# Two tokens side by side instead of sixteen: the layout of the one-hot rows that the PEER pick weights are built from

## The chip, the cores and the metric

The kernel runs on one core of a Trainium2 chip. The metric is the time of one execution in device microseconds; the kernel before takes 2791.45 us (median of 3 runs, 2790.54 to 2801.08). Engines are named as the profile names them: PE is TensorE's matmuls, PEld its weight loads, DVE is VectorE, ACT is ScalarE, POOL is GpSimd, SP issues DMAs.

## The reference, cut to what matters

Two layers run over 384 tokens: 256 prompt tokens and 128 sample tokens. Each layer is attention followed by a PEER block, and the change lies in the PEER block of the prompt tokens.

```python
def one(xb):                                   # xb: tokens x 1024
    q = (xb @ w_pq).reshape(m, 8, 2, 64)
    s1 = einsum('nhd,hkd->nhk', q[:, :, 0], k1); s2 = einsum('nhd,hkd->nhk', q[:, :, 1], k2)
    v1, i1 = top_k(s1, 16); v2, i2 = top_k(s2, 16)
    cand = v1[..., :, None] + v2[..., None, :]
    cid = i1[..., :, None] * 128 + i2[..., None, :]
    sc, pick = top_k(cand.reshape(m, 8, 256), 16)
    eid = take_along_axis(cid.reshape(m, 8, 256), pick)   # 8 x 16 experts of 16384 for each token
    g = softmax(sc)
    a = gelu(einsum('nhkd,nd->nhk', u_tab[eid], xb))
    return einsum('nhk,nhkd->nd', g * a, v_tab[eid])
```

An expert's number is `eid = 128*i1 + i2`. For the 256 prompt tokens the kernel computes all 16384 experts densely and multiplies them with a weight matrix G (expert x token) that is zero where a token did not pick an expert. G is what the changed code builds.

## The kernel before

**The PEER block of a layer.** The sample tokens gather their rows: 128 indirect DMAs of rows of `peer_u` and 128 of `peer_v`, 128 x 1024 fp32 each (`gather_slots`, L841), each followed by one DVE instruction on the row (L846 for u, L849 for v); four row buffers. The prompt tokens go through all experts in 64 steps `pb` of 256 experts. A step has a first half (`plain_first` L877 for pb 0 to 15, `first` for the others): load 1 MB of u, multiply with the normed tokens, gelu. Its second half (`second`) multiplies the result by G on DVE (L933), loads 1 MB of v and accumulates the product in four PSUM banks. Most operands are split in two fp32r parts on ACT (L149) and DVE (L152), and every product takes three matmuls (L155 to L157).

**The build of G.** `build(es, tb)` makes G for two groups `es` of 16 columns of `i2`-values (32 columns) and one block `tb` of 16 tokens (`TB = 16`). There are 8 groups, so 4 x 16 = 64 builds in a layer. The 128 picks of a token (8 heads x 16) lie on the 128 partitions. For one token, the left operand A[p, i] is 1 where pick p has `i1 = i`, the right operand B[p, j] is the gate of pick p where `i2 = j`, and A^T B is the token's 128 x 32 piece of G, one matmul (two in fact, B having a high and a low fp16 part: index `i` of the loop). So a build is 32 pairs of a weight load (128 columns of A, fp16) and a matmul that streams 32 columns of B (L910), all into one PSUM bank, which two ACT instructions copy to G (L913).

A is made in one of two ways, given by the table `ACT_ROWS`: in 30 of the 64 builds of a layer by ACT, one `Square` of (2 x id - 2 x i1) per token (L889, 16 of them) and one `Relu` over all (L891), in 34 by one DVE comparison over all 16 tokens (L895). B is always made by DVE: one comparison (L897) and two multiplications by the two parts of the gate (L900).

**The layout.** `iota_r` holds the ids 0 to 127, each repeated 16 times (`[128, 128, TB]`). A tile made by DVE has the shape (id, token): one token's ids are 16 fp16 elements apart, 32 bytes. B always has this shape. A tile made by ACT has the shape (token, id), so one token's 128 ids lie side by side, but ACT reads the ids themselves from `iota_r[:, :, 0]`, 32 bytes apart. The pattern with which a weight load or a matmul reads A and B is `A[:, :, t0 + t]` and `Bt[:, i, :, t0 + t]`.

**What runs around it.** Builds of group pair (0, 1) come first, between the `plain_first` steps 10 to 15. Then `run` walks the 64 steps; in each it does `second(pb)`, the `first` of a later step, then the builds that `BUILDS` gives (pair (2, 3): 16 builds over steps 8 to 15, two per step; (4, 5) and (6, 7): one per step over steps 16 to 47), then some gathered rows (48 by step 16, 256 by step 64). The Tile framework's scheduler decides the final order of the instructions on each engine, and inserts the waits. Tiles: A has two halves in `As`, B two buffers, the PSUM tile of a build is one of three (`at`).

Of the kernel before, what the change touches and what calls it, by code (L numbers as in the profile page):

```python
# [76 lines left out]
def tile_stream_encoder(ctx: ExitStack, tc: tile.TileContext, I, O, stop=None):  # L77
# [546 lines left out]
    def pick(l, hT, hS, kp, dst, after):  # L624
# [95 lines left out]
        def ids(t):  # L720
# [96 lines left out]
    class Experts:  # L817
# [62 lines left out]

        def build(self, es, tb):

            ts = slice(tb * TB, tb * TB + TB)
            dst, L, n = self.dst, self.L, 16 * len(es)
            A = self.As[:, tb % 2 * 1024:tb % 2 * 1024 + 1024].bitcast(F16)
            if tb in ACT_ROWS[es[0]]:

# [17 lines left out]
            m = TB if n * TB <= 512 else TB // 2  # L905
            for t0 in range(0, TB, m):
                ps = at(f"{L}_gp{es[0]}{tb}{t0}")
                for t in range(m):
                    for i in range(2):
# [1 line left out]
                pv = ps[:, :m * n].rearrange("p (t i) -> p i t", t=m)
                for j, e in enumerate(es):
                    S.activation(self.G[e][:, :, tb * TB + t0:tb * TB + t0 + m], pv[:, j * 16:j * 16 + 16], AF.Copy,  # L913
                                 scale=1.0 / GSCALE)
# [164 lines left out]
```

## Time and profile before

| what | value |
|---|---|
| time, median of 3 runs | 2791.45 us (2790.54 to 2801.08) |
| the profiled execution | 2796.06 us, its span 2794.3 us |
| PE busy / DVE busy / ACT busy / POOL busy | 2632.9 / 2170.9 / 1552.8 / 833.0 us |
| mean granted clock of TensorE | 0.962 |
| moved by DMA | 640.14 MB, mean 229 GB/s |

Busy time is the union of an engine's instructions; a matmul's record includes the time it takes to drain, so a busy PE is not a PE at its peak. The profile divides the span in 40 slices of 70 us. The PEER block of the first layer lies at about 430 to 1400 us, that of the second at about 1820 to 2794 us; builds run from 535 to 1220 us and from 1923 to 2610 us.

### The profile page before, as it was taken

Reading aid. Unit: us, or ns where it says so; the run is one execution under the profiler, and the core shown is the slowest. Engines: PE = TensorE matmul, PEld = TensorE weight load, DVE = VectorE, ACT = ScalarE, POOL = GpSimd, SP = SyncE. Lnnn points to the kernel's source line nnn. Section 1 sums busy time; section 2 is a strip of 40 time slices with the busy share of each in tenths; the row PEclk is TensorE's granted clock in tenths of the full one; section 3 lists DMA queues with packets and bytes.
Section 4 is the critical chain, followed back from the end, with each engine's and each line's share of the span. In section 5 each row is a group of like instructions: output and inputs, shape, how many; then the busy total and the mean of one; then the engine's idle time right before and its main releaser. Section 6 shows DMA issues by size and latency. Waiting matters only on the chain.

```text
span 2794.3 us, 45301 instructions
## 1 busy us (share of the span) xinstructions
PE 2632.9 (94%) x17316; PEld 2239.0 (80%) x17316; DVE 2170.9 (78%) x4346; ACT 1552.8 (56%) x2594; POOL 833.0 (30%) x585
## 2 busy tenths in 40 slices
PE   7989998898999999999988989979989999999998
PEld 6767876786789999997876669767857899999987
DVE  6754569967789899998767445698677898989986
ACT  4344333463778888843434443325627788888433
POOL 1000101224334454465210001012243344445651
PEclk9999999999899999999999989999899999999999
DMA  4243532567689888899633343326686888888995
GB/s 164 87 126 109 148 115 76 221 247 291 228 292 331 308 318 317 318 334 353 232 106 103 114 153 115 106 91 234 226 294 233 293 328 307 323 310 320 350 343 198
DMA packets 172010, 640.14 MB, mean 229 GB/s; under 512 B 20880, under 2 KB 37008, under 8 KB 139024
## 3 DMA queue, kind: packets, MB, share of 16 engines
q1 hardware_dynamic: 98064, 368.77, 37.1%
q0 software_dynamic: 73728, 268.47, 26.6%
q8 instruction: 136, 2.23, 0.3%
q14 instruction: 82, 0.67, 0.1%
HBM read 631.48 MB, written 5.70 MB: 228 GB/s over the span
## 4 chain that ended last, share of the span: by engine, by line
PE 62%; DVE 14%; issue 10%; DMA 7%; POOL 4%; ACT 3%; POOLq 0%; SPq 0%; ACTq 0%; DVEq 0%
DMA l0x_row<-in_peer_v_dram,l0e_eid 4%; PE l1x_gp L910 3%; PE l0x_gp L910 3%; PE l1x_acc L156 3%; PE l1x_H L155 3%; PE l1x_acc L157 3%; PE l1x_acc L155 3%; PE l1x_H L157 3%; PE l1x_H L156 3%; PE l0x_acc L156 2%; PE l0x_H L155 2%; PE l0x_acc L157 2%; PE l0x_acc L155 2%; PE l0x_H L157 2%; PE l0x_H L156 2%
## 5 line engine op out<-in xcount | busy, mean ns | idle before, releaser
L841 POOL DMA_INDIRECT l1x_row<-in_peer_v_dram,l1e_eid x128 | 219.6, 1715 | 186.5 <-DVE x_s L849 171.7
L841 POOL DMA_INDIRECT l0x_row<-in_peer_v_dram,l0e_eid x128 | 218.4, 1706 | 187.9 <-DVE x_s L849 166.4
L841 POOL DMA_INDIRECT l1x_row<-in_peer_u_dram,l1e_eid x128 | 161.5, 1261 | 332.9 <-DVE l1x_row L846 295.1
L841 POOL DMA_INDIRECT l0x_row<-in_peer_u_dram,l0e_eid x128 | 161.2, 1259 | 329.3 <-DVE l0x_row L846 289.1
L157 PE MATMUL l0x_H<-l0e_h,l0x_u_l 128*128 128x256 f32 x768 | 219.7, 286 | 4.5 <-DVE l0x_u_l L152 4.3
L155 PE MATMUL l1x_H<-l1e_h,l1x_u_h 128*128 128x256 f32 x768 | 221.8, 289 | 0.0
L155 PE MATMUL l0x_H<-l0e_h,l0x_u_h 128*128 128x256 f32 x768 | 221.7, 289 | 0.0
L157 PE MATMUL l1x_H<-l1e_h,l1x_u_l 128*128 128x256 f32 x768 | 219.3, 285 | 2.5 <-DVE l1x_u_l L152 2.4
L156 PE MATMUL l1x_H<-l1e_h,l1x_u_h 128*128 128x256 f32 x768 | 218.9, 285 | 0.0
L156 PE MATMUL l0x_H<-l0e_h,l0x_u_h 128*128 128x256 f32 x768 | 218.8, 285 | 0.0
L889 ACT ACTIVATE l0x_As<-iota_r,l0e_ni 128x128 f16<-128x128 f16 x480 | 216.8, 541 | 0.0
L889 ACT ACTIVATE l1x_As<-iota_r,l1e_ni 128x128 f16<-128x128 f16 x480 | 216.6, 538 | 0.0
L156 PE MATMUL l0x_acc<-l0x_v_l,l0x_ch 128*128 128x512 f32 x464 | 184.1, 397 | 9.9 <-DVE l0x_v_l L152 9.9
L156 PE MATMUL l1x_acc<-l1x_v_l,l1x_ch 128*128 128x512 f32 x464 | 184.6, 398 | 9.2 <-DVE l1x_v_l L152 9.2
L155 PE MATMUL l1x_acc<-l1x_v_h,l1x_ch 128*128 128x512 f32 x464 | 184.7, 398 | 4.4 <-ACT l1x_v_h L149 4.4
L155 PE MATMUL l0x_acc<-l0x_v_h,l0x_ch 128*128 128x512 f32 x464 | 184.2, 397 | 3.8 <-ACT l0x_v_h L149 3.8
L157 PE MATMUL l1x_acc<-l1x_v_h,l1x_cl 128*128 128x512 f32 x464 | 182.7, 394 | 0.0
L849 DVE SCALAR_TENSOR_TENSOR x_s<-l0x_row,l0x_act,x_s 128x1024 f32<-128x1024 f32 x128 | 165.4, 1292 | 21.9 <-DMA l0x_row<-in_peer_v_dram,l0e_eid 21.2
L157 PE MATMUL l0x_acc<-l0x_v_h,l0x_cl 128*128 128x512 f32 x464 | 182.0, 392 | 0.0
L849 DVE SCALAR_TENSOR_TENSOR x_s<-l1x_row,l1x_act,x_s 128x1024 f32<-128x1024 f32 x128 | 164.0, 1281 | 20.0 <-DMA l1x_row<-in_peer_v_dram,l1e_eid 19.0
L149 ACT ACTIVATE l0x_v_h<-l0x_v 128x1024 fp32r<-128x1024 f32 x116 | 121.3, 1052 | 95.3 <-DMA l0x_v<-in_peer_vt_dram 50.8
L149 ACT ACTIVATE l1x_v_h<-l1x_v 128x1024 fp32r<-128x1024 f32 x116 | 121.2, 1052 | 95.2 <-DMA l1x_v<-in_peer_vt_dram 51.2
(528 smaller groups left out, 7693.6 us busy)
## 6 DMA issues: line engine op xcount, KB each, us to landing
l0x_u_raw<-in_peer_ut_dram SPq DMA_DIRECT2D x64, 1024.0 KB
l0x_v<-in_peer_vt_dram SPq DMA_DIRECT2D x64, 1024.0 KB
l1x_u_raw<-in_peer_ut_dram SPq DMA_DIRECT2D x64, 1024.0 KB
l1x_v<-in_peer_vt_dram SPq DMA_DIRECT2D x64, 1024.0 KB
l_g_raw<-in_w_in_dram SPq DMA_DIRECT2D x16, 1024.0 KB
l_pa_raw<-in_w_in_dram SPq DMA_DIRECT2D x8, 1024.0 KB
l_kbT<-in_cache_b_kT_dram SPq DMA_DIRECT2D x16, 512.0 KB
l_cvb<-in_cache_b_vt_dram SPq DMA_DIRECT2D x16, 512.0 KB
```

The lines of the kernel that those rows point to most:

```text
L149: op = S.activation(hi, src, AF.Copy)
L155: PE.matmul(out, lh, rh, start=start, stop=False)
L156: PE.matmul(out, lh, rl, start=False, stop=False)
L157: PE.matmul(out, ll, rh, start=False, stop=stop)
L841: G.indirect_dma_start(out=row, out_offset=None, in_=self.tables[which], in_offset=bass.IndirectOffsetOnAxis(ap=self.dst["eid"][:, s:s + 1 ...
L849: V.scalar_tensor_tensor(x[2], row, act[:, s:s + 1], x[2], op0=ALU.mult, op1=ALU.add)
L889: S.activation(A[:, t * 128:t * 128 + 128], iota_r[:, :, 0], AF.Square, scale=2.0, bias=dst["ni1"][:, tb * TB + t:tb * TB + t + 1])
L910: PE.matmul(ps[:, t * n:t * n + n], A[:, :, t0 + t], Bt[:, i, :, t0 + t], start=i == 0, stop=i == 1)
```

## The change

The ids are kept in three tiles: `iota_1`, each id once; `iota_2`, each id twice; `iota_16`, ids 0 to 15, sixteen times each, for one comparison in `ids` that read them from `iota_r`. POOL fills them at the start, 128 + 256 + 256 elements in place of 2048. DVE's A and B now have the shape (pair of tokens, id, token of the pair): one token's ids are 2 fp16 elements apart, 4 bytes. The ids are read as one run of 256 (or 64) elements, once for each of the 8 pairs; the tokens' own ids or gates (`pairs`) as runs of 2 elements, each run read 128 (or 32) times. ACT reads its ids from `iota_1`, side by side, and writes as before. The number of instructions and their shapes stay the same. The loop over halves of a block falls away; with 32 columns it ran once.

```diff
-    iota_r = cp.tile([128, 128, TB], F16, name="iota_r")
-    G.tensor_copy(iota_r, iota[:, :, None].to_broadcast([128, 128, TB]))
+    iota_1 = cp.tile([128, 128], F16, name="iota_1")
+    G.tensor_copy(iota_1, iota)
+    iota_2 = cp.tile([128, 128, 2], F16, name="iota_2")
+    G.tensor_copy(iota_2, iota[:, :, None].to_broadcast([128, 128, 2]))
+    iota_16 = cp.tile([128, 16, 16], F16, name="iota_16")
+    G.tensor_copy(iota_16, iota[:, 0:16, None].to_broadcast([128, 16, 16]))
...
-            V.tensor_tensor(ge, every(row[:, :, None, :]), every(iota_r[:, None, 0:16, :]), ALU.is_ge)
+            V.tensor_tensor(ge, every(row[:, :, None, :]), every(iota_16[:, None]), ALU.is_ge)
...
+            def pairs(v, m):
+                return (v[:, tb * TB:tb * TB + TB].rearrange("p (c a) -> p c a", a=2)[:, :, None, :]
+                        .to_broadcast([128, NP, m, 2]))
             if tb in ACT_ROWS[es[0]]:
                 for t in range(TB):
-                    S.activation(A[:, t * 128:t * 128 + 128], iota_r[:, :, 0], AF.Square, scale=2.0,
+                    S.activation(A[:, t * 128:t * 128 + 128], iota_1, AF.Square, scale=2.0,
                                  bias=dst["ni1"][:, tb * TB + t:tb * TB + t + 1])
...
             else:
-                A = carve(A, (128, TB))
-                V.tensor_tensor(A, iota_r, dst["i12"][:, 0, None, ts].to_broadcast([128, 128, TB]), ALU.is_equal)
-            Bt = carve(self.gp.tile([128, 2 * 48 * TB], F16, name=f"{L}_B{es[0]}{tb}", tag="B"), (2, n, TB))
-            V.tensor_tensor(Bt[:, 1], iota_r[:, es[0] * 16:es[0] * 16 + n, :],
-                            dst["i12"][:, 1, None, ts].to_broadcast([128, n, TB]), ALU.is_equal)
+                A = carve(A, (NP, 128, 2))
+                V.tensor_tensor(A, iota_2[:, None].to_broadcast([128, NP, 128, 2]), pairs(dst["i12"][:, 0], 128),
+                                ALU.is_equal)
+                first = [A[:, t // 2, :, t % 2] for t in range(TB)]
+            Bt = carve(self.gp.tile([128, 2 * 48 * TB], F16, name=f"{L}_B{es[0]}{tb}", tag="B"), (2, NP, n, 2))
+            V.tensor_tensor(Bt[:, 1], iota_2[:, None, es[0] * 16:es[0] * 16 + n, :].to_broadcast([128, NP, n, 2]),
+                            pairs(dst["i12"][:, 1], n), ALU.is_equal)
             for i in range(2):
-                V.tensor_tensor(Bt[:, i], Bt[:, 1], dst["gp"][:, i, None, ts].to_broadcast([128, n, TB]), ALU.mult)
+                V.tensor_tensor(Bt[:, i], Bt[:, 1], pairs(dst["gp"][:, i], n), ALU.mult)
...
-                        PE.matmul(ps[:, t * n:t * n + n], A[:, :, t0 + t], Bt[:, i, :, t0 + t], start=i == 0, stop=i == 1)
+                    PE.matmul(ps[:, t * n:t * n + n], first[t], Bt[:, i, t // 2, :, t % 2], start=i == 0, stop=i == 1)
```

The scheduler's order of instructions hardly moves. The first place is ACT's queue among the builds of pair (0, 1) in the first layer. `l0x_As` is A, `iota_r` and then `iota` are the ids, `l0x_G<-l0x_gp` the copy of a build's PSUM bank to G, `l0e_co` the gelu of a step, and "x5" five instructions of one form in a row. Before:

```order
L891 ACTIVATE l0x_As_4340<-l0x_As_4340 128x2048
L913 ACTIVATE l0x_G_4346<-l0x_gp_4560 128x16x16
L913 ACTIVATE l0x_G_4347<-l0x_gp_4560 128x16x16
L913 ACTIVATE l0x_G_4346<-l0x_gp_4600 128x16x16
L913 ACTIVATE l0x_G_4347<-l0x_gp_4600 128x16x16
L889 ACTIVATE l0x_As_4340<-iota_r,l0e_ni_3046 128x128 x5
L879 ACTIVATE l0e_co_3040<-l0x_H_4635 128x512
L889 ACTIVATE l0x_As_4340<-iota_r,l0e_ni_3046 128x128 x3
```

And the same place of the changed kernel:

```order
L901 ACTIVATE l0x_As_4344<-l0x_As_4344 128x2048
L924 ACTIVATE l0x_G_4350<-l0x_gp_4564 128x16x16
L924 ACTIVATE l0x_G_4351<-l0x_gp_4564 128x16x16
L899 ACTIVATE l0x_As_4344<-iota_89,l0e_ni_3050 128x128
L924 ACTIVATE l0x_G_4350<-l0x_gp_4604 128x16x16
L924 ACTIVATE l0x_G_4351<-l0x_gp_4604 128x16x16
L899 ACTIVATE l0x_As_4344<-iota_89,l0e_ni_3050 128x128 x5
L884 ACTIVATE l0e_co_3044<-l0x_H_4639 128x512
L899 ACTIVATE l0x_As_4344<-iota_89,l0e_ni_3050 128x128 x2
```

One of the eight `Square` instructions of this stretch moves ahead of two copies to G; nothing else changes. The second place is PE's queue in the same stage, a build's first pairs. `l0x_gp<-l0x_B,l0x_As` is a build's matmul, `l0x_H` one of the plain matmuls of a step. Before:

```order
L910 LDWEIGHTS l0x_As_4340
L910 MATMUL l0x_gp_5088<-l0x_B_5084,l0x_As_4340 128x32
L910 LDWEIGHTS l0x_As_4340
L910 MATMUL l0x_gp_5088<-l0x_B_5084,l0x_As_4340 128x32
L910 LDWEIGHTS l0x_As_4340
```

And now:

```order
L921 LDWEIGHTS l0x_As_4344
L921 MATMUL l0x_gp_5092<-l0x_B_5088,l0x_As_4344 128x32
L882 MATMUL l0x_H_5167<-l0x_hf,l0x_u_raw 128x256
L921 LDWEIGHTS l0x_As_4344
L921 MATMUL l0x_gp_5092<-l0x_B_5088,l0x_As_4344 128x32
```

One plain matmul of a later step now stands between the pairs of this build; the number of pairs is the same, 2048 in a layer.

## Rows read from the trace of the kernel before

**Rows 1.** The page: the span, the busy time of each engine, and in 40 slices of the span the busy tenths of PE and POOL and the granted clock.
```profile
span 2794.3 us, 45301 instructions
PE 2632.9 (94%) x17316; PEld 2239.0 (80%) x17316; DVE 2170.9 (78%) x4346; ACT 1552.8 (56%) x2594; POOL 833.0 (30%) x585
PE   7989998898999999999988989979989999999998
POOL 1000101224334454465210001012243344445651
PEclk9999999999899999999999989999899999999999
```

**Rows 2.** Stretches of the two PEER blocks: start and end, length, busy time of PE, PEld, DVE, ACT and POOL, granted clock, DMA share, GB/s.
```profile
535.00:640.00 105.00, 101.92 (x797) 89.58 (x796) 77.17 (x134) 70.75 (x143) 27.46 (x26) 0.93 0.70 258
640.00:700.00 60.00, 50.22 (x214) 33.70 (x213) 46.42 (x70) 13.96 (x19) 29.25 (x22) 0.89 0.88 323
700.00:800.00 100.00, 98.89 (x732) 77.83 (x731) 74.65 (x127) 65.65 (x130) 35.39 (x28) 0.90 0.70 248
...
830.00:1190.00 360.00, 360.00 (x2825) 329.14 (x2825) 330.44 (x407) 304.21 (x510) 171.27 (x109) 1.00 0.87 317
1230.00:1355.00 125.00, 117.66 (x739) 104.54 (x738) 111.81 (x103) 50.44 (x59) 78.34 (x45) 1.00 0.94 350
...
2220.00:2580.00 360.00, 360.00 (x2814) 329.01 (x2813) 329.07 (x404) 305.85 (x513) 170.68 (x110) 1.00 0.87 318
```

**Rows 3.** Who PE waited for in 530 to 1400 us: us in total, times, the longest.
```profile
PE l0x_acc L156 <- DVE l0x_v_l L152: 9.9, 7, 4.3
PE l0x_H L157 <- DVE l0x_u_l L152: 4.3, 5, 1.7
PE l0x_acc L155 <- ACT l0x_v_h L149: 3.8, 1, 3.8
PE l0x_gp L910 <- ACT l0x_As L891: 3.5, 6, 0.9
```

**Rows 4.** The build's instructions in the first layer, grouped by line: busy us, mean ns of one, idle time before them.
```profile
L889 ACT ACTIVATE l0x_As<-iota_r,l0e_ni 128x128 f16<-128x128 f16 x480 | 216.8, 541 | 0.0
L910 PE MATMUL l0x_gp<-l0x_B,l0x_As 128*128 128x32 f16 x2048 | 140.5, 245 | 4.2 <-ACT l0x_As L891 3.5 <-DVE l0x_B L900 0.7
L900 DVE TENSOR_TENSOR l0x_B<-l0x_B,l0e_gp 128x512 f16<-128x512 f16 x128 | 51.5, 418 | 0.1
L895 DVE TENSOR_TENSOR l0x_As<-iota_r,l0e_i 128x2048 f16<-128x2048 f16 x34 | 41.6, 1224 | 24.6 <-PE l0x_gp L910 24.6
L897 DVE TENSOR_TENSOR l0x_B<-iota_r,l0e_i 128x512 f16<-128x512 f16 x64 | 26.8, 418 | 7.8 <-PE l0x_gp L910 7.7
```

**Rows 5.** Matmuls on PE in order of time: start, us, name, count. A row of x32 is one whole build (the one at 830.02 with A from DVE, the one at 1096.14 with A from ACT), x1 a single matmul.
```profile
543.91 0.38 PE L877 MATMUL l0x_H<-l0x_hf,l0x_u_raw 128*128 128x256 f32 x1
544.13 0.23 PE L910 MATMUL l0x_gp<-l0x_B,l0x_As 128*128 128x32 f16 x1
...
830.02 2.31 PE L910 MATMUL l0x_gp<-l0x_B,l0x_As 128*128 128x32 f16 x32
...
834.00 0.28 PE L155 MATMUL l0x_H<-l0e_h,l0x_u_h 128*128 128x256 f32 x1
834.12 0.28 PE L156 MATMUL l0x_H<-l0e_h,l0x_u_h 128*128 128x256 f32 x1
...
1096.14 2.11 PE L910 MATMUL l0x_gp<-l0x_B,l0x_As 128*128 128x32 f16 x32
```

**Rows 6.** Durations of one matmul or weight load in ns, smallest/median/largest: the build's, and three whose moving columns lie side by side (512 and 272 columns bf16, 8 columns fp32).
```profile
L910 PEld LDWEIGHTS <-l0x_As x2048: 95/146/183, 535.1 to 1217.8; 128*128 128x128 f16 x187
L910 PE MATMUL l0x_gp<-l0x_B,l0x_As x2048: 217/242/264, 535.3 to 1217.9; 128*128 128x32 f16 x187
L425 PEld LDWEIGHTS <-identb x12: 95/96/96, 107.7 to 1533.6; 128*128 128x128 bf16 x12
L490 PE MATMUL l_ss<-l_tk_nm,l_spread x16: 279/279/434, 178.1 to 1603.1; 128*128 128x272 bf16 x16
L455 PE MATMUL l_pw<-cst,l_wsp x4: 170/214/256, 156.1 to 1546.1; 128*128 128x8 f32 x4
```

**Rows 7.** ACT on 128 elements side by side, grouped by line: with a bias per partition and an accumulated sum (L394), and a plain copy (L752, ns smallest/median/largest).
```profile
L394 ACT ACTIVATE l_ex<-l_sc,l_sm_st 128x128 f32<-128x128 f32 x16 | 5.8, 365 | 10.1 <-DVE l_sm_st L393 10.0
...
L752 ACT ACTIVATE l0p_fi<-l0p_e x4: 309/309/310, 514.1 to 529.8; 128x128 f32<-128x128 f16 x4
```

**Rows 8.** DVE's tensor by tensor in fp32, grouped by line. L701 with 48 elements reads both inputs in runs of 2, with 64 elements in runs of 8; L310 reads one input as single elements repeated 64 times; L933 reads and writes 512 elements in rows.
```profile
L933 DVE TENSOR_TENSOR l0x_co<-l0x_co,l0x_G 128x512 f32<-128x512 f32 x48 | 32.9, 686 | 9.9 <-ACT l0x_co L927 8.3 <-ACT l0x_G L913 1.4
L310 DVE TENSOR_TENSOR l_R<-l_R,l_rn_y 128x768 f32<-128x768 f32 x6 | 5.7, 953 | 0.1
L701 DVE TENSOR_TENSOR l0p_cand<-l0p_v 128x64 f32<-128x64 f32 x6 | 1.3, 217 | 0.0
L701 DVE TENSOR_TENSOR l0p_cand<-l0p_v 128x48 f32<-128x48 f32 x3 | 0.6, 203 | 0.0
```

**Rows 9.** Who DVE waited for in 830 to 1190 us and, the last row, in 1230 to 1355 us: us in total, times, the longest.
```profile
DVE l0x_u_l L152 <- ACT l0x_u_h L149: 12.6, 19, 1.4
DVE l0x_co L933 <- ACT l0x_co L927: 8.3, 9, 1.9
...
DVE x_s L849 <- DMA l0x_row<-in_peer_v_dram,l0e_eid: 13.0, 11, 2.3
```

More of the change, by code (lines that the diff above doesn't have):

```diff
@@ L881, in build @@
         def build(self, es, tb):
-            ts = slice(tb * TB, tb * TB + TB)
-            dst, L, n = self.dst, self.L, 16 * len(es)
+            dst, L, n, NP = self.dst, self.L, 16 * len(es), TB // 2
             A = self.As[:, tb % 2 * 1024:tb % 2 * 1024 + 1024].bitcast(F16)
+            def pairs(v, m):
+                return (v[:, tb * TB:tb * TB + TB].rearrange("p (c a) -> p c a", a=2)[:, :, None, :]
+                        .to_broadcast([128, NP, m, 2]))
             if tb in ACT_ROWS[es[0]]:
                 for t in range(TB):
-                    S.activation(A[:, t * 128:t * 128 + 128], iota_r[:, :, 0], AF.Square, scale=2.0,
+                    S.activation(A[:, t * 128:t * 128 + 128], iota_1, AF.Square, scale=2.0,
                                  bias=dst["ni1"][:, tb * TB + t:tb * TB + t + 1])
                 S.activation(A, A, AF.Relu, scale=-1.0, bias=1.0)
-                A = carve(A, (TB, 128)).rearrange("p t i -> p i t")
-            else:
-                A = carve(A, (128, TB))
-                V.tensor_tensor(A, iota_r, dst["i12"][:, 0, None, ts].to_broadcast([128, 128, TB]), ALU.is_equal)
-            Bt = carve(self.gp.tile([128, 2 * 48 * TB], F16, name=f"{L}_B{es[0]}{tb}", tag="B"), (2, n, TB))
-            V.tensor_tensor(Bt[:, 1], iota_r[:, es[0] * 16:es[0] * 16 + n, :],
-                            dst["i12"][:, 1, None, ts].to_broadcast([128, n, TB]), ALU.is_equal)
+                A = carve(A, (TB, 128))
+                first = [A[:, t, :] for t in range(TB)]
+            else:
+                A = carve(A, (NP, 128, 2))
[5 more added lines that the diff above has]
+                            pairs(dst["i12"][:, 1], n), ALU.is_equal)
             for i in range(2):
-                V.tensor_tensor(Bt[:, i], Bt[:, 1], dst["gp"][:, i, None, ts].to_broadcast([128, n, TB]), ALU.mult)
+                V.tensor_tensor(Bt[:, i], Bt[:, 1], pairs(dst["gp"][:, i], n), ALU.mult)
             for e in es:
@@ L904, in build @@
                     self.G[e] = carve(g, (16, TP))
[L905 to L909, printed above, removed]
-                        PE.matmul(ps[:, t * n:t * n + n], A[:, :, t0 + t], Bt[:, i, :, t0 + t], start=i == 0, stop=i == 1)
[L911 to L914, printed above, removed]
+            ps = at(f"{L}_gp{es[0]}{tb}")
+            for t in range(TB):
+                for i in range(2):
+                    PE.matmul(ps[:, t * n:t * n + n], first[t], Bt[:, i, t // 2, :, t % 2], start=i == 0, stop=i == 1)
+            pv = ps[:, :TB * n].rearrange("p (t i) -> p i t", t=TB)
+            for j, e in enumerate(es):
+                S.activation(self.G[e][:, :, tb * TB:tb * TB + TB], pv[:, j * 16:j * 16 + 16], AF.Copy,
+                             scale=1.0 / GSCALE)
         def first(self, pb):
```

## Prediction, made before the run

> **What bounds the kernel now.** I began with the page: PE is busy 94% of the span, DVE 78%, ACT 56% [rows 1]. A share over the whole span says little here, so the second view was the stretches of the PEER blocks. Call A the builds of pair (0, 1), 535 to 640 us; B those of pair (2, 3), 700 to 800 us; C those of the last two pairs, 830 to 1190 us. Only in these stretches does the changed code run. PE is busy 101.9 of 105 us in A, 98.9 of 100 in B, 360 of 360 in C [rows 2]. The third view, PE's waits, guards against reading a record's drain as work: over the whole block they make some 21 us, and only 3.5 of them are for an A of the builds [rows 3]. So in A, B and C the end is set by how fast PE takes its instructions, and time taken off PE there can come off the span.
>
> How far depends on what comes next. In B it is far off: DVE 75 of 100 us, ACT 66, DMA share 0.70. In C it is near: DVE 330 of 360 us, DMA share 0.87 at 317 GB/s, while in 1230 to 1355 us, where no builds run, DMA reaches 0.94 and 350 GB/s [rows 2] and DVE waits 13.0 us for gathered rows [rows 9]. Between A and B lies a stretch with DMA 0.88 and PE busy only 50 of 60 us [rows 2]: what A gains is partly waited away there.
>
> **PE: the matmuls of a build.** A build is 32 pairs of a weight load and a matmul of 32 columns. Two pieces of PE's order of time show a build undisturbed: 2.31 us where DVE made A, 2.11 us where ACT did [rows 5]. The last matmul's own 0.24 us [rows 6] is mostly drain, so a pair takes (2.31 − 0.24)/31 = 67 ns or (2.11 − 0.24)/31 = 60 ns. The two differ only in A's layout, so 32-byte steps of the weights cost about 7 ns a pair. B has 32-byte steps in both.
>
> What would 32 columns cost if they lay close together? Durations first: 8 columns take 170 ns at the least, 272 take 279 [rows 6], hence 0.41 ns per column and 180 ns for 32. A matmul of a build that starts behind a plain one took 230 ns [rows 5], 50 ns more, or 1.6 ns more for each of its columns. So the columns of B seem to come in at about 2 ns each, 64 ns for 32, which is the step of 60 to 67. Weight loads say the same: 146 ns at the median, against 95 for 128 two-byte columns side by side [rows 6]. The change leaves 4 bytes between the columns. That has a row: the fp32r products read 4 bytes per column and start 120 ns apart with 256 columns [rows 5], 0.42 × 256 = 107 and 13 for the rest. So 4-byte steps should be read at full rate, for A too.
>
> A pair would then take 13 ns for the columns and 13 for the rest, 26 ns. That is the lower bound; the upper is the 60 of today's better build. Weight loads come one per 13 ns of columns here and one per 107 in the fp32r products, so less of them can hide. I take 34 ns, nearer the lower bound, because the row it is worked from has the same alternation of load and matmul. In A and B, 11 of 16 builds have A from DVE (`ACT_ROWS`), a mean of 65 ns: each build saves 32 × 31 = 0.99 us, 15.9 us per stage.
>
> - B: all of it, 15.9 us.
> - A: 0.8 of it, 12.7 us, my choice between all and half, since the stretch behind it has PE idle for 10 of 60 us and transfers near their most.
> - C: 32 builds would save PE 32 × 32 × 29 = 29 us, 360 to 331, about DVE's 330. DVE won't run without gaps; it waits 12.6 us for ACT's rounding of u and 8.3 for ACT's gelu [rows 9]. By the transfers, 360 × 317/350 = 326 us are the least. I take 346, a saving of 14 us (DVE at 95% where it is at 92% now); bounds 5 and 25.
>
> The sum is 42.6 us a layer. The second layer's stage C is busy like the first's [rows 2], so 85 us in two layers.
>
> **ACT.** 960 `Square` take 541 ns each [rows 4]. With the ids side by side the nearest rows are 309 ns (a copy) and 365 ns (with a bias per partition and a sum) [rows 7]. That is 170 to 220 us off ACT's 1553, yet ACT is busy 304 of 360 us in C and less elsewhere [rows 2]. What can reach the end is a share of PE's 3.5 us and of DVE's 12.6 and 8.3 us of waits for ACT, since ACT queues these behind `Square`. I count it as what lets DVE run at 95% in C, and nothing else. If that cover were gone, C would save 5 us instead of 14.
>
> **DVE.** Counts and sizes stay. Now 512 elements of B take 418 ns and 2048 of A 1224 ns [rows 4], while 512 fp32 take 686 [rows 8]: the fp16 forms run two elements a tick. I expect the same after, since every operand still has runs of at least 2 neighbouring fp16. Two fp32 rows back this: runs of 2 give 203 ns for 48 elements, where runs of 8 give 217 for 64, and a single element repeated 64 times runs at (953 − 203)/(768 − 48) = 1.04 ns an element, the rate of rows [rows 8]. No row has fp16 in runs of 2, so the bounds are 0 and the loss of the second element per tick, which is a rival below.
>
> [...]
>
> **POOL and the rest.** The ids are filled in the first slice, 640 elements instead of 2048, where POOL is busy one tenth [rows 1]; the comparison in `ids` keeps its size. Nothing is taken for them. One `Square` ahead of two copies to G, and one plain matmul between two pairs, shift things by one `Square`, 0.54 us [rows 4], and free no buffer earlier.
>
> **The clock.** [...] It fell to 0.89 in the stretch where PE waits for transfers. Shorter builds may give more such waits; I take nothing, and up to 5 us a layer in the range.
>
> **The sum.** The profiled execution took 2796.06 us. Less 85 it is 2711; the median of the runs is 4.6 below that execution, so 2706.
>
> **The rivals.**
>
> - Only part arrives. PE gains as above, but A's gain is lost in the transfers behind it and C stays at DVE's pace: B's 15.9 and 2 us a layer, 2 × 18 = 36, so 2755. For it: DVE's 92% and DMA 0.87 in C. Against: there DVE's idle time is spent on waits for ACT, which gets faster.
> - A floor in PE's step. The pair stays at 60 ns, whatever B's layout, and only the 68 builds with A from DVE gain 32 × 7 = 0.22 us: 15 us, of which 14 count, so 2777. For it: 60 is reached in a build with A side by side. Against: the durations of 230 and 180 ns, which differ with B's layout. [...]
> - DVE loses its second element per tick. A would take 686 + 1.043 × 1536 = 2288 ns, B 686. Per layer 34 × 1.06 + 192 × 0.27 = 88 us more on DVE. In C (12 builds with A from DVE) it is 12 × 1.06 + 96 × 0.27 = 39 us against 30 idle, in A and B 25 us each against 25 to 28 idle. It decides once DVE needs some 30 us more in C: with its waits, C becomes about 385 us and A and B give back their gain, so near +27 a layer, 2791 + 54 = 2845.
>
> **The numbers.** The chances: 0.70 for the forecast, 0.09 for the part, 0.12 for the floor, 0.09 for DVE's loss. The forecast's own range comes from a step of 26 ns with 25 us in C (16 + 20 + 25 = 61 a layer, 2669) to one of 45 ns with 5 us in C (8 + 10 + 5 = 23 a layer, 2745). The range for 8 in 10 goes to the floor's time, 2668 to 2780. A difference of 0.5%, 14 us, is about what a measurement of this kernel tells from none: faster has the forecast, the part and a third of the floor, 0.83; same the rest of the floor and a little, 0.09; slower 0.08.
>
> **What would show it.** Right: a build of 32 pairs in about 1.2 us; matmuls of a build near 180 ns and loads near 100; `Square` at 310 to 365 ns; the comparison for A still near 1.22 us and B's three near 0.42; PE below 100% busy in C with DVE near 95% and DMA above 0.87; B some 16 us shorter. Wrong by the floor: builds of 2.1 us whoever made A. Wrong by DVE: 2.3 us and 0.69 us for A and B, and PE waiting for both. Wrong in size: short builds, but C as long as before.

## Result: 2662.6 us, more gain than forecast

The changed kernel takes 2662.56 us (median of 4 runs, 2657.18 to 2671.48) against 2791.75 us before; the ratio is 0.9533, 95% interval 0.950 to 0.957. The forecast was 2706 us with a range from 2668 to 2780, and the result lies 5 us below that range: the direction and the forecast's account of PE held, the size did not. The page of the profiled execution (span, busy time of the engines, and in 40 slices the busy tenths of PE and POOL and the granted clock) answers to [rows 1]:

```profile
span 2661.2 us, 45317 instructions
PE 2468.2 (93%) x17316; PEld 2070.9 (78%) x17316; DVE 2158.2 (81%) x4346; ACT 1415.6 (53%) x2594; POOL 896.8 (34%) x587
PE   7889998898999999999999999988889999999998
POOL 1100010144445566566210000002344455666551
PEclk9999999899999999999999999989999999999999
```

PE's busy time fell by 164.7 us, the span by 133.1. The instructions of the build, grouped by line (busy us, mean ns of one, idle time before them), answer to [rows 4]; L899 is the `Square`, L906 VectorE's A, L910 and L913 the three instructions on B, L921 the matmul and the weight load:

```profile
L899 ACT ACTIVATE l0x_As<-iota,l0e_ni 128x128 f16<-128x128 f16 x480 | 149.7, 394 | 14.0 <-DVE l0x_B L913 7.9 <-PE l0x_gp L921 6.1
L921 PE MATMUL l0x_gp<-l0x_B,l0x_As 128*128 128x32 f16 x2048 | 62.3, 177 | 11.2 <-DVE l0x_B L913 10.5 <-ACT l0x_As L901 0.6
L921 PEld LDWEIGHTS <-l0x_As 128*128 128x128 f16 x2048 | 57.0, 96 | 26.4 <-issue 13.5 <-DVE l0x_B L913 7.9 <-ACT l0x_As L901 3.0
L906 DVE TENSOR_TENSOR l0x_As<-iota,l0e_i 128x2048 f16<-128x2048 f16 x34 | 41.5, 1221 | 1.4 <-PE l0x_gp L921 1.4
L910 DVE TENSOR_TENSOR l0x_B<-iota,l0e_i 128x512 f16<-128x512 f16 x64 | 26.4, 420 | 0.3 <-PE l0x_gp L921 0.3
L913 DVE TENSOR_TENSOR l0x_B<-l0x_B,l0e_gp 128x512 f16<-128x512 f16 x128 | 51.6, 418 | 0.1
```

A matmul takes 177 ns in place of 245, VectorE's instructions are what they were, and a new wait stands ahead of the matmuls: 10.5 us for B. The order of time on PE, with two whole builds (the first with A from ScalarE, the second from VectorE), answers to [rows 5]:

```profile
830.61 0.97 PE L921 MATMUL l0x_gp<-l0x_B,l0x_As 128*128 128x32 f16 x32
...
855.61 0.97 PE L921 MATMUL l0x_gp<-l0x_B,l0x_As 128*128 128x32 f16 x32
```

A build now takes 0.97 us, whoever makes A: a step of (0.97 − 0.18)/31 = 25 ns where it was 60 and 67.

To see where the time went, the block is cut at the builds themselves, from the first pair of a stage to its last: A, what lies between, B, C with the few microseconds ahead of it, and the rest of the block. The same cuts in the first layer of the kernel before and of the changed one (start and end, length, busy time of PE, PEld, DVE, ACT, POOL, granted clock, DMA share, GB/s):

```profile
535.10:622.80 87.70, 84.62 (x718) 75.02 (x717) 62.22 (x111) 56.30 (x117) 26.53 (x25) 0.92 0.75 277
622.80:691.90 69.10, 59.32 (x223) 42.28 (x221) 54.09 (x82) 24.81 (x39) 27.57 (x21) 0.93 0.77 282
691.90:790.70 98.80, 97.69 (x744) 74.77 (x744) 74.31 (x121) 60.17 (x117) 35.21 (x27) 0.90 0.72 255
790.70:1217.80 427.10, 427.10 (x3332) 390.54 (x3331) 387.19 (x479) 354.60 (x596) 200.18 (x128) 1.00 0.86 313
1217.80:1398.60 180.80, 172.38 (x1061) 152.51 (x1059) 152.62 (x143) 78.49 (x94) 86.56 (x50) 1.00 0.83 305
```
```profile
532.90:600.90 68.00, 61.70 (x723) 52.64 (x721) 61.60 (x111) 45.97 (x114) 28.59 (x24) 1.00 0.92 343
600.90:668.20 67.30, 59.21 (x223) 42.39 (x220) 53.73 (x83) 23.77 (x40) 30.31 (x23) 0.92 0.84 309
668.20:745.50 77.30, 70.72 (x746) 49.67 (x745) 70.31 (x115) 50.79 (x119) 33.04 (x24) 0.97 0.83 296
745.50:1143.40 397.90, 392.49 (x3335) 353.49 (x3331) 381.93 (x482) 307.14 (x593) 224.96 (x129) 0.99 0.92 337
1143.40:1327.70 184.30, 174.63 (x1061) 153.43 (x1057) 156.98 (x147) 78.93 (x95) 88.79 (x53) 0.99 0.84 309
```

| stretch | forecast saving, a layer | first layer | second layer |
|---|---|---|---|
| A | 12.7 | 87.7 − 68.0 = 19.7 | 19.2 |
| between | 0 | 1.8 | 1.8 |
| B | 15.9 | 98.8 − 77.3 = 21.5 | 22.4 |
| C | 14 | 427.1 − 397.9 = 29.2 | 29.6 |
| the rest | 0 | −3.5 | −10.5 |
| sum | 42.6 | 68.7 | 62.5 |

Two columns of the rows deserve a look. The granted clock of A and B rose from 0.92 and 0.90 to 1.00 and 0.97, with PE less busy than before. And in C PE is busy 392.5 of 397.9 us: after the loss of 35 us of its work it is still nearly full.

### The profile page after: what moved, and what is told of

It reads as the page before. It is cut to its first block, busy times and chain, and to the rows that moved or that the text cites. A ratio compares the mean times of both kernels' runs of the same rounds, so it can differ in the third digit from the quotient of the medians.

```text
span 2661.2 us, 45317 instructions
## 1 busy us (share of the span) xinstructions
PE 2468.2 (93%) x17316; PEld 2070.9 (78%) x17316; DVE 2158.2 (81%) x4346; ACT 1415.6 (53%) x2594; POOL 896.8 (34%) x587
## 4 chain that ended last, share of the span: by engine, by line
PE 34%; issue 21%; DVE 20%; POOL 13%; DMA 9%; ACT 2%; POOLq 0%; SPq 0%; DVEq 0%; ACTq 0%
POOL l0x_row L846 7%; POOL l1x_row L846 6%; DMA l0x_row<-in_peer_v_dram,l0e_eid 4%; DMA l1x_row<-in_peer_v_dram,l1e_eid 3%; DVE x_s L854 2%; PE l1x_acc L161 1%; PE l1x_acc L162 1%; PE l_g_ps L160 1%; PE l1x_acc L160 1%; PE l_g_ps L161 1%; PE l_g_ps L162 1%; PE l1x_H L160 1%; PE l1x_H L162 1%; PE l1x_H L161 1%; PE l_pa_ps L160 1%
## 5 line engine op out<-in xcount | busy, mean ns | idle before, releaser
L846 POOL DMA_INDIRECT l1x_row<-in_peer_v_dram,l1e_eid x128 | 240.4, 1878 | 150.0 <-DVE x_s L854 131.7
L846 POOL DMA_INDIRECT l0x_row<-in_peer_v_dram,l0e_eid x128 | 236.1, 1845 | 153.0 <-DVE x_s L854 128.0
L846 POOL DMA_INDIRECT l1x_row<-in_peer_u_dram,l1e_eid x128 | 174.6, 1364 | 272.2 <-DVE l1x_row L851 231.0
L846 POOL DMA_INDIRECT l0x_row<-in_peer_u_dram,l0e_eid x128 | 174.3, 1361 | 265.6 <-DVE l0x_row L851 226.3
L161 PE MATMUL l1x_acc<-l1x_v_l,l1x_ch 128*128 128x512 f32 x464 | 186.7, 402 | 13.6 <-DVE l1x_v_l L157 13.4
L851 DVE SCALAR_TENSOR_TENSOR l1x_row<-l1x_row,l1e_xn 128x1024 f32<-128x1024 f32 x128 | 155.4, 1225 | 31.3 <-DMA l1x_row<-in_peer_u_dram,l1e_eid 30.8
L851 DVE SCALAR_TENSOR_TENSOR l0x_row<-l0x_row,l0e_xn 128x1024 f32<-128x1024 f32 x128 | 155.5, 1225 | 29.7 <-DMA l0x_row<-in_peer_u_dram,l0e_eid 28.3
```

The lines of the kernel that those rows point to most:

```text
L161: PE.matmul(out, lh, rl, start=False, stop=False)
L846: G.indirect_dma_start(out=row, out_offset=None, in_=self.tables[which], in_offset=bass.IndirectOffsetOnAxis(ap=self.dst["eid"][:, s:s + 1 ...
L851: V.scalar_tensor_tensor(row, row, 1.0, self.xn_s, op0=ALU.mult, op1=ALU.mult, accum_out=act[:, s:s + 1])
```

## Experiments

Each kernel ran beside the kernel before; times are medians. What the scheduler does with the gathered rows (the 256 DVE instructions of a layer that follow the indirect DMAs) turned out to matter: an edit of the builds moves them. The table gives how many stand ahead of steps 16 and 32 in DVE's queue. The kernel before has 77 and 132 like the changed one.

| kernel | us | ratio to before (95%) | rows ahead of step 16, 32 |
|---|---|---|---|
| changed | 2662.6 | 0.953 (0.950 to 0.957) | 77, 132 |
| ids alone | 2763.8 | 0.991 (0.988 to 0.994) | 77, 132 |
| layout alone | 2691.8 | 0.964 (0.962 to 0.967) | 74, 130 |
| B in pairs, A by 8 | 2690.1 (one run) | | 77, 132 |
| widths | 2722.2 (one run) | | 70, 124 |
| token rows | 2802.1 | 1.003 (1.001 to 1.006) | 48, 113 |
| half the pairs | 2608.7 | 0.933 (0.929 to 0.936) | 69, 121 |
| pairs twice | 2799.9 | 1.003 (1.001 to 1.005) | 99, 159 |
| more DVE | 2643.2 | 0.945 (0.943 to 0.948) | 69, 122 |
| rows later | 2644.7 | 0.947 (0.946 to 0.949) | 62, 113 |
| small copy | 2665.6 | 0.955 (0.954 to 0.957) | 79, 134 |

### The ids alone

```diff
+    iota_1 = cp.tile([128, 128], F16, name="iota_1")
+    G.tensor_copy(iota_1, iota)
...
-                    S.activation(A[:, t * 128:t * 128 + 128], iota_r[:, :, 0], AF.Square, scale=2.0,
+                    S.activation(A[:, t * 128:t * 128 + 128], iota_1, AF.Square, scale=2.0,
```

> The kernel before, with only ScalarE's ids side by side (a tile of 128 ids beside the interleaved one); A and B keep their 16 interleaved tokens. Theory 1, the time follows PE's step in the builds and ScalarE is off the path: Square takes 393 ns in place of 541 as in the changed kernel, steps stay at 60 and 66 ns, and the time falls by no more than PE's waits for these tiles, 0 to 7 us, 2785 to 2792 us. Theory 2, the 15 us a layer that the forecast missed in the last two group pairs came from ScalarE's shorter queue: 20 to 40 us less, 2750 to 2770 us.

It gave some 26 us by the ratio (34.7 us between the two profiled executions), the size of theory 2, but not where theory 2 had it. The same cuts of its first layer (A, B, C):

```profile
535.70:617.40 81.70, 80.62 (x719) 72.86 (x718) 62.30 (x111) 46.73 (x114) 26.80 (x25) 0.98 0.79 291
...
684.70:779.90 95.20, 95.12 (x745) 72.58 (x745) 74.36 (x121) 50.80 (x116) 34.21 (x27) 0.93 0.74 265
779.90:1205.50 425.60, 425.60 (x3331) 389.05 (x3329) 390.63 (x481) 315.73 (x596) 197.34 (x130) 1.00 0.87 316
```

C, with 39 us less work on ACT, is 1.5 us shorter; PE has no gap there and ACT cannot help. A is 6.0 us shorter and B 3.6, and PE's own busy time fell by 4.0 and 2.6 with the steps of the builds unchanged. What changed there is the clock: 0.92 to 0.98 in A, 0.90 to 0.93 in B. Over both layers of the profiled pair A and B give 22.1 of the 34.7 us; the rest of the block gives 7.9 and the stretch between A and B 3.1.

Where the clock fell can be read in the kernel before. Two stretches around a fall (columns as above), and PE's order of time ahead of it:

```profile
564.00:569.20 5.20, 4.86 (x69) 4.67 (x69) 3.42 (x7) 1.59 (x5) 0.94 (x1) 1.00 0.78 265
569.20:572.60 3.40, 3.40 (x27) 2.79 (x26) 2.38 (x6) 3.33 (x9) 0.75 (x1) 0.51 0.63 201
```
```profile
559.63 4.48 PE L877 MATMUL l0x_H<-l0x_hf,l0x_u_raw 128*128 128x256 f32 x20
564.46 4.18 PE L910 MATMUL l0x_gp<-l0x_B,l0x_As 128*128 128x32 f16 x64 [0.34 <-ACT l0x_As L891]
568.46 2.98 PE L877 MATMUL l0x_H<-l0x_hf,l0x_u_raw 128*128 128x256 f32 x8
```

At 569.2 us the granted clock drops from 1.00 to 0.51, behind two whole builds in a row (64 pairs, 4.18 us), the first of them after 0.34 us of waiting for an A of ScalarE. In the record PE was busy 4.86 of 5.20 us. A and B of the kernel before have 18 falls of the clock in the two layers; 16 of them come in the second of two such builds in a row or less than 1 us behind it. But not every such pair of builds is followed by a fall: with the ids alone the same 64 pairs start at 564.89 us, and the clock stays at 1.00 (columns as above):

```profile
565.00:575.00 10.00, 10.00 (x114) 9.52 (x114) 7.19 (x14) 6.07 (x20) 1.87 (x2) 1.00 0.79 308
```

So what ScalarE's ids have to do with the clock is not shown. Weighting each stretch's missing clock by its length gives what the low level can have cost: 0.08 × 87.7 + 0.10 × 98.8 = 16.9 us in the first layer; 8.3 with the ids alone; 2.3 in the changed kernel. With the second layer (0.89 of 91.2 us and 0.90 of 99.1 before) it is 36.8, 18.3 and 8.2 us. So about 18 us of what the ids gave can be the clock; this is bookkeeping, not a run in which the clock alone differed.

In the changed kernel the clock falls four times from A on in the first layer's block, each time in a wait of PE of 2.1 to 3.4 us or less than 1 us behind one, as between A and B (3.1 us); in the second layer there are four falls within A and B (0.95 and 0.97 there), with waits of 0.9 to 3.0 us at or ahead of them. The fall between A and B:

```profile
650.70:655.80 5.10, 1.61 (x6) 0.76 (x5) 2.47 (x5) 2.04 (x3) 3.72 (x4) 1.00 1.00 402
655.80:666.00 10.20, 6.02 (x14) 4.77 (x15) 8.45 (x12) 0.48 (x1) 4.81 (x3) 0.50 0.86 328
```

### Five widths in one run

```diff
-            dst, L, n, NP = self.dst, self.L, 16 * len(es), TB // 2
+            dst, L, n, W = self.dst, self.L, 16 * len(es), (16, 8, 4, 2, 1)[tb % 5]
+            NP = TB // W
...
-                A = carve(A, (NP, 128, 2))
-                V.tensor_tensor(A, iota_2[:, None].to_broadcast([128, NP, 128, 2]), pairs(dst["i12"][:, 0], 128),
+                A = carve(A, (NP, 128, W))
+                V.tensor_tensor(A, iota_r[:, None, :, 0:W].to_broadcast([128, NP, 128, W]), pairs(dst["i12"][:, 0], 128),
...
```

> The changed kernel with the interleave set by the block number: 16, 8, 4, 2 and 1 tokens side by side in turn, so that one run has columns 32, 16, 8, 4 and 2 bytes apart for the matmuls of B, and for the weight loads where VectorE made A (by ScalarE always 2 bytes). All ids are read from the old interleaved tile. Theory 1, what the prediction used (about 2 ns a column at 32 bytes, full rate at 4): a step of 60 to 67 ns at 32 bytes and 25 at 4 and 2; between them it falls with the distance, 30 to 45 ns at 16 bytes, 25 at 8. Theory 2, a surcharge for every distance above 4 bytes alike: 60 to 67 at 16 and 8 bytes too. VectorE's comparison for A: 1.22 us for 16 to 2 tokens; for 1 token 2.29 us if a repeated single fp16 loses the second element of a tick, 1.22 if not.

The builds one after the other, with 16, 8, 4, 2, 1 and 16 tokens interleaved (A from ACT, ACT, DVE, ACT, ACT, DVE):

```profile
781.03 2.10 PE L920 MATMUL l0x_gp<-l0x_B,l0x_As 128*128 128x32 f16 x32
794.25 2.08 PE L920 MATMUL l0x_gp<-l0x_B,l0x_As 128*128 128x32 f16 x32
807.44 1.24 PE L920 MATMUL l0x_gp<-l0x_B,l0x_As 128*128 128x32 f16 x32
819.83 0.97 PE L920 MATMUL l0x_gp<-l0x_B,l0x_As 128*128 128x32 f16 x32
831.95 0.96 PE L920 MATMUL l0x_gp<-l0x_B,l0x_As 128*128 128x32 f16 x32
844.06 2.34 PE L920 MATMUL l0x_gp<-l0x_B,l0x_As 128*128 128x32 f16 x32
```

So 2 and 4 bytes cost the same, 25 ns a step; 8 bytes (1.24 − 0.19)/31 = 34; 16 bytes cost all that 32 do, 60. Theory 1 missed both distances between (8 bytes are not at full rate, 16 are no cheaper than 32); theory 2 is right at 16 and wrong at 8.

This run reads VectorE's ids from the old tile, where a run of 2 ids is one 4-byte word and the next lies 32 bytes on. The comparison for B with 4, 2 and 1 tokens interleaved:

```profile
784.60 0.42 DVE L909 TENSOR_TENSOR l0x_B<-iota_r,l0e_i 128x512 f16<-128x512 f16 x1
...
797.59 0.63 DVE L909 TENSOR_TENSOR l0x_B<-iota_r,l0e_i 128x512 f16<-128x512 f16 x1
...
811.33 1.13 DVE L909 TENSOR_TENSOR l0x_B<-iota_r,l0e_i 128x512 f16<-128x512 f16 x1
```

One 4-byte word at a time with hops costs 0.63 in place of 0.42 us, one fp16 at a time 1.13; the comparison for A takes 2.0 and 3.9 us with 2 and 1 tokens (4.1 at the longest), where at most 1.22 and 2.29 were expected. The changed kernel escapes this: its ids lie side by side, and the other input, one word read again and again, costs nothing (0.42 us at L910).

### Every token's ids side by side

```diff
-                A = carve(A, (NP, 128, 2))
-                V.tensor_tensor(A, iota_2[:, None].to_broadcast([128, NP, 128, 2]), pairs(dst["i12"][:, 0], 128),
+                A = carve(A, (TB, 128))
+                V.tensor_tensor(A, iota_1[:, None].to_broadcast([128, TB, 128]), each(dst["i12"][:, 0], 128),
...
```

> The changed kernel with every token's ids side by side (no interleave) also where VectorE makes A and B: the inputs per token are then one fp16 repeated 128 or 32 times. PE's step 25 ns as with pairs. Theory 1, VectorE loses its second element per tick: 2.29 us for A and 0.69 for each instruction on B, 88 us more VectorE work a layer; it binds in all three stages, +35, +20 and +19 us a layer, about 2810 us. Theory 2, it keeps its rate: 2662 us, and pairs would not be needed.

Theory 1, within 8 us. VectorE's A and two of the three instructions on B by line, and its stage C (columns as above):

```profile
L903 DVE TENSOR_TENSOR l0x_As<-iota,l0e_i 128x2048 f16<-128x2048 f16 x34 | 77.7, 2286 | 1.8 <-PE l0x_gp L918 1.8
L910 DVE TENSOR_TENSOR l0x_B<-l0x_B,l0e_gp 128x512 f16<-128x512 f16 x128 | 86.1, 685 | 0.0
```
```profile
754.70:1206.60 451.90, 413.73 (x3324) 371.06 (x3323) 428.39 (x517) 311.80 (x589) 218.69 (x136) 0.94 0.87 307
```

With a single repeated fp16 the comparison for A takes 2286 ns in place of 1221, where the prediction's rival had 2288, and an instruction on B 685 in place of 418. PE's matmuls take 177 ns as in the changed kernel (64.6 us in all against 62.3), and the whole gain is lost again: C is 54 us longer than in the changed kernel, for 39 us more of VectorE's work on the builds there (its busy time is 46 us longer), with the clock at 0.94, although its gathered rows stand later (what that is worth comes below). That the total fits theory 1 so well is luck: the three stages were to be 35, 20 and 19 us longer, and in the first layer C is 54 us longer, B 6 us longer and A 5 us shorter. But VectorE's loss takes the gain, and that is why two tokens stand side by side and not one.

### B in pairs, A by 8

```diff
-                A = carve(A, (NP, 128, 2))
+                A = carve(A, (2, 128, 8))
...
-                first = [A[:, t // 2, :, t % 2] for t in range(TB)]
+                first = [A[:, t // 8, :, t % 8] for t in range(TB)]
```

> The changed kernel with the A that VectorE makes interleaved by 8 tokens (16 bytes apart, a distance that cost the full 60 ns in the run with widths), B in pairs. Theory 1, as the prediction read it, A's distance is worth 7 ns a pair and B's the rest: a step of about 32 ns in builds with A from VectorE, under 15 us on the time, 2662 to 2677 us. Theory 2, the slower of the two operands sets the step alone: 60 ns there, 68 x 32 x 35 ns = 76 us of PE, 2715 to 2740 us.

A build with A from VectorE takes 2.13 us, one with A from ScalarE 0.97, and C is (columns as above):

```profile
797.92 2.13 PE L924 MATMUL l0x_gp<-l0x_B,l0x_As 128*128 128x32 f16 x32
```
```profile
761.00:1163.70 402.70, 402.70 (x3322) 366.27 (x3322) 384.65 (x483) 312.24 (x594) 216.15 (x131) 1.00 0.92 337
```

The step is 60 ns, theory 2: one operand far apart is enough, and the 7 ns that the prediction had read as the price of A's distance were only what a second one adds. But the time was wrong: not 53 to 78 us over the changed kernel but 28. This kernel has the row order of the kernel before and of the changed one, so the three divide the gain. From ids alone to this kernel PE loses 60 × 32 × 35 + 68 × 32 × 6 ns = 80 us of work and the span falls by 2759.6 − 2688.3 = 71. From here to the changed kernel it loses 68 × 32 × 35 ns = 76 us more, and the span falls by 27. The first half came through nearly whole, with some help of the clock (0.98 in both A and B here). Of the second a third did, because PE then waits: in the first layer it is idle here for 1.0 us in A, 1.2 in B and none in C, in the changed kernel for 6.3, 6.6 and 5.4.

### Half the pairs, and more VectorE work

Two runs on what binds after the change. The first leaves out the matmuls of the gate's low part:

```diff
-                for i in range(2):
-                    PE.matmul(ps[:, t * n:t * n + n], first[t], Bt[:, i, t // 2, :, t % 2], start=i == 0, stop=i == 1)
+                PE.matmul(ps[:, t * n:t * n + n], first[t], Bt[:, 0, t // 2, :, t % 2], start=True, stop=True)
```

> The changed kernel, leaving out the matmuls of the gate's low part (so G lacks that part): 16 pairs of load and matmul per build in place of 32, all else as it is. It takes 16 x 25 ns = 0.4 us of PE per build, 25.6 us a layer. Theory 1, PE still sets the pace of the last two group pairs after the change: 32 x 0.4 = 13 us a layer there and little in the first two, 25 to 32 us in all, about 2635 us. Theory 2, VectorE or the transfers bind after the change: under 8 us, 2655 to 2662.

The second makes the comparison for B twice (L910 written two times in a row).

> The changed kernel with VectorE's comparison for B done twice: 0.42 us more per build, 26.8 us a layer, 13.4 of it in the last two group pairs, where VectorE was busy 370.6 of 385.5 us. Theory 1, PE still sets the pace and VectorE's idle time takes most of it: 10 to 30 us in all, 2672 to 2692 us. Theory 2, VectorE binds after the change, as the prediction had it for the last two pairs: nearly all of it comes through, 45 to 54 us, 2707 to 2716 us.

Both went past their theories. Half the pairs gave 54 us where only 51 us of PE's work were taken away, and more work on VectorE made the kernel 19 us faster. C and the rest of the block in the second (columns as above):

```profile
746.90:1140.10 393.20, 391.09 (x3331) 353.20 (x3329) 379.78 (x511) 307.72 (x593) 208.45 (x120) 0.99 0.91 329
1140.10:1327.30 187.20, 176.57 (x1059) 155.65 (x1056) 175.29 (x164) 78.14 (x96) 111.59 (x69) 0.97 0.92 345
```

VectorE is not busier in C than in the changed kernel (379.8 against 381.9 us) although its builds give it 13.4 us more to do there: it does fewer gathered rows, and more of them in the rest of the block (POOL 111.6 us there against 88.8). In both runs the scheduler had moved the rows to a later place.

### The place of the gathered rows

A short fill of B's first half, which the multiplications then overwrite, moves the rows further; a copy of 64 elements in the same place does not. (`V.memset(Bt[:, 0], 0.0)` in the one, `V.tensor_copy(Bt[:, 0, 0:1], Bt[:, 1, 0:1])` in the other, behind the comparison for B.)

> The run with more VectorE work was faster than the changed kernel, and in it the scheduler had put the gathered rows later on VectorE: of 256 row instructions a layer 69 stood ahead of step 16 and 122 ahead of step 32, where the changed kernel has 77 and 132. Here the changed kernel gets one short fill of B's first half ahead of the two multiplications (which overwrite it), and the scheduler's order then has 62 and 113. Theory 1, the place of the rows decides: as fast as the run with more VectorE work or faster, 2630 to 2648 us. Theory 2, something else in that run gave the gain: 2660 to 2675 us, the fill's own time added.

> The control for the run with the fill: the changed kernel with a copy of a 16th of B (64 elements) in its place, again one more VectorE instruction per build, which leaves the gathered rows where the changed kernel has them or a little earlier (79 ahead of step 16, 134 ahead of step 32). Theory 1, the place of the rows decides: no gain, 2660 to 2685 us. Theory 2, one more instruction per build on VectorE helps in itself, by whatever way: 2630 to 2650 us.

2644.7 and 2665.6 us: the place of the rows decides, 18 us for 15 rows fewer ahead of step 16. Who PE waited for in B, in the changed kernel and with the rows later, and C with the rows later (columns as above):

```profile
PE l0x_gp L921 <- DVE l0x_B L913: 6.5, 6, 3.4
```
```profile
PE l0x_gp L922 <- DVE l0x_B L914: 0.7, 1, 0.7
738.80:1131.10 392.30, 389.98 (x3327) 352.64 (x3327) 381.54 (x521) 310.30 (x595) 174.32 (x124) 1.00 0.91 335
```

In B the builds of the changed kernel wait for a B that stands behind gathered rows in VectorE's queue, and VectorE itself waits 8.9 us there for the transfers of four rows (2.2 us with the rows later). Three things follow. More work on VectorE does not by itself make the kernel slower: the run with the comparison twice gives it 27 us a layer more than the changed kernel, this one 17 (64 fills of 272 ns), and both are faster; in both, rows have moved behind C. But neither shows that VectorE does not bind in C: its busy time there did not grow (379.8 and 381.5 us against 381.9), and in all three kernels PE (99%) and VectorE (96 to 97%) are both nearly full; which of the two sets C's length is not separated. Half the pairs, whose rows stand as in the run with the comparison twice, is 35 us faster than that run, but it also has those 27 us a layer less of VectorE's work: 35 us is the most that its 51 us of PE can be worth. And this is a version that beats both kernels, by 0.7% against the changed one.

### The layout alone, and pairs twice

```diff
-                    S.activation(A[:, t * 128:t * 128 + 128], iota_1, AF.Square, scale=2.0,
+                    S.activation(A[:, t * 128:t * 128 + 128], iota_r[:, :, 0], AF.Square, scale=2.0,
```

> The changed kernel with ScalarE's ids read as before, from a tile that holds them 28 bytes apart (it takes the place of the 32 bytes, which did not fit beside the pairs): Square near 541 ns, VectorE's layout and PE's 25 ns as in the changed kernel. The ids alone had given about 26 us, all of it in the first two group pairs. Theory 1, that gain was time that TensorE ran at its lower clock behind two long builds in a row, and builds at 25 ns bring that gain by themselves: only 5 to 20 us over the changed kernel, 2667 to 2682 us, the last two pairs as in the changed kernel (385 us a layer). Theory 2, the two parts add up: 26 us over it, about 2688 us.

29 us over the changed kernel, near theory 2, but 5.8 us a layer of it lie ahead of the builds (89.8 against 84.0 us in the first layer, VectorE busy 88.6 against 83.1), where, to make room, the comparison in `ids` read a repeated single fp16. Without them it is 18 us, the upper end of theory 1, and the place is that of neither. A and B are as short as in the changed kernel; C is longer (columns as above; then who DVE waited for there):

```profile
751.80:1162.40 410.60, 397.32 (x3330) 354.05 (x3329) 382.84 (x484) 349.93 (x596) 199.55 (x131) 0.99 0.90 326
```
```profile
DVE l0x_u_l L157 <- ACT l0x_u_h L154: 8.5, 11, 1.3
```

With the step at 25 ns C leans on ACT: with `Square` at 540 ns its rounding of u comes late for VectorE (8.5 us), and VectorE's parts of u and v late for PE (3.5 and 6.6 us, where the changed kernel has 3.1 for v alone). So the ids gave their time mostly by way of A and B when PE was slow (22.1 of 34.7 us; the expectation had all of it there), and 13 us a layer in C now that it is fast.

The other run issues all pairs twice (`for i in (0, 1, 0, 1)`).

> The changed kernel with every token's two matmuls issued twice (the second round starts the sum anew, so G is the same): 64 pairs of 25 ns, 1.6 us a build, close to the 1.8 to 2.0 us that a build took before, but with its columns twice as dense in time. It adds 0.8 us x 128 = 102 us of PE. Theory 1, TensorE's clock fell before because pairs at 60 ns keep it busy in the record and do little: the low stretches in the first two group pairs stay at 30 us or less in both layers (75 before, 20 in the changed kernel), and the time comes to 2662 + 80 to 105, 2742 to 2767 us. Theory 2, the length of a build made the clock fall: 60 us or more at the low level, and a time near the kernel before less 0.3 us x 128, 2750 to 2790 us with the granted clock at 0.93 or less there.

2799.9 us, above both theories. The scheduler moved 99 rows ahead of step 16 here, so its time can't be compared with the others'. On the clock it lies between: by its clocks of 0.96 and 0.93 in the first layer's A and B and 0.96 and 0.92 in the second's, 21.5 us, against 36.8 before and 8.2 in the changed kernel. Whether the slow step or the length of the builds makes the clock fall stays open.

## Why the prediction was right or wrong

- **PE's mechanism: right.** Builds are 0.97 us where about 1.2 was forecast, matmuls 177 ns (about 180), loads 96 (near 100), and the step no longer depends on who makes A. One part of it was wrong: I read 7 ns of the step as the price of A's distance and the rest as B's, but either operand far apart makes the 60 ns alone.
- **The step's size: mis-sized.** I took 34 ns between the bounds of 26 and 60; it is 25. At 25, A and B are worth 32 × 40 × 16 ns = 20.5 us each in place of 15.9. The reason I gave for going above the bound, that weight loads hide less behind short matmuls, was my estimate, and no run shows it: with a load in each pair the step is 25 ns, where the bound was 26.
- **A's share: not settled.** I had let 0.8 of it through, for the transfers behind it. A is 19.7 and 19.2 us shorter, nearly all of 20.5; but its clock rose too, which the sum did not have. From the run with the ids alone, where the clock had risen already, A gains 81.7 − 68.0 = 13.7 us, 0.67 of 20.5, and 10.3 us in the second layer.
- **C: the step that failed.** I capped C at 346 of 360 us, because VectorE, busy 330, would not get past 95%. That share was nearly right: 381.9 of 397.9 us are 96%. What it was a share of was wrong. The window of 360 us holds 27.5 of the 32 builds whose 29 us I took off PE; over the whole 427.1 us the same cap is 387.2/0.95 = 407.6 us, a saving of 19.5 in place of 14. VectorE's busy time in the stage then fell from 387.2 to 381.9 us, 5.6 us more, and its share by one point, the last 4. That C's length is also 427 − 29 = 398 us, PE alone at my own step, is chance: at 25 ns PE alone would be near 389, an estimate (427.1 less 32 × 42 ns for each of 12 builds and 32 × 35 ns for each of 20).
- **VectorE's waits: taken as lasting.** Its idle time in C was 39.9 us before, 31 of them waits for ScalarE (the longest are in [rows 9]), and I kept half of it. In the changed kernel none of these waits is left; 14 of the 16 us idle are waits for gathered rows. With the ids alone, 39 us less work on ScalarE and PE's step as before, 29 us of them stay; with the layout alone 13. So most of them came from PE's step. Who VectorE waited for longest in C, before, with the ids alone and in the changed kernel:

```profile
DVE l0x_u_l L152 <- ACT l0x_u_h L149: 17.6, 23, 2.4
DVE l0x_u_l L154 <- ACT l0x_u_h L151: 18.6, 29, 1.3
DVE x_s L854 <- DMA l0x_row<-in_peer_v_dram,l0e_eid: 10.8, 11, 2.7
```

- **The transfers in C**: their share went from 0.86 to 0.92, 337 GB/s. That they cost nothing there is not shown, since VectorE's waits for rows grew from 7.5 to 14.2 us.
- **ScalarE: priced at nothing, wrong.** Its ids are worth 26 us alone and at most 18 on top of the layout. The sentence that C would save 5 in place of 14 without this cover pointed the right way: without it C saves 427.1 − 410.6 = 16.5 of the 29. `Square` is 394 ns, above both rows that I had bounded it by.
- **The clock: left out.** I gave it 5 us a layer in the range and nothing in the sum, and feared it would get worse. It got better by up to (36.8 − 8.2)/2 = 14 us a layer: most of its falls (16 of 18 in A and B) had come with two builds in a row, and I took time from the builds. With the larger step (4.6 us in each of A and B) that is more than the 12.6 us by which A and B together went past the forecast; part of it is lost to PE's waits (idle 3.1 us in A and 1.1 in B before, 6.3 and 6.6 now).
- **The rest of the block: not foreseen.** It lost 3.5 and 10.5 us, with PE's busy time there up by 2 to 4 us and the clock at 0.99 and 0.98; why the second layer lost more was not tried.
- **VectorE: right**, at 1221, 420 and 418 ns. The rival's price was right as well (2286 and 685 ns), but it is paid for single elements, not for pairs. One row that I leaned on backs this less than I took it to: the first input of L701 with 48 elements is single values read twice, not runs of 2 [rows 8].
- **The floor: refuted**, by a step of 25 ns.

In the first layer the forecast fell short by 7.0 us in A, 1.8 behind it, 5.6 in B and 15.2 in C, 29.6 us, and was 3.5 too high in the rest: 26 us a layer, half of it in C.

## What to carry to other kernels

Lay out what PE reads so that neighbours in the stream are at most 4 bytes apart, for both operands: here the step was 25 ns so, and one operand at 16 bytes or more set it at 60. When a stage is bound by PE, do not take the other engines' waits there as lasting: VectorE's waits for ScalarE in C went from 31 us to none once PE's step was short. Take a bound from the whole stage to which the saving belongs, not from a window inside it. And look at the granted clock of the stage, which rose here from 0.90 to 0.92 up to 0.97 to 1.00. Where a scheduler fills an engine's queue with side work, compare kernels only after looking at where that work went.

## What was not expected of the hardware

- PE's step for 32 columns with a weight load each: 25 ns at distances of 2 and 4 bytes, 34 at 8, 60 at 16 and 32; 60 as well if only the weights lie 16 bytes apart, 67 if both lie 32 apart.
- The granted clock fell from 1.00 to 0.51 behind 4 us of matmuls that the record shows as nearly gapless (PE busy 4.86 of 5.20 us), and did not behind the same matmuls in the run with the ids alone.
- VectorE on fp16: a run of 2 read again and again 0.42 us for 512 elements, a run of 2 at a hop of 32 bytes 0.63, a single element repeated 0.69.
